# State space output of a hybrid decoder block: unmasked half-height products, put in feature order by DMA

## The chip, the cores and the metric

One core of one Trainium2 chip runs the whole kernel. The metric is the device time of one execution in microseconds (us), as the median of three runs. TensorE is the matrix engine (PE in the rows, its weight loads PEld), VectorE is DVE, ScalarE is ACT, GpSimd is POOL. SyncE (SP) issues every DMA of this kernel, in one queue.

## What is computed

A decoder block over 272 positions (16 meta tokens and 256 real ones) of width 2048. The part that matters is the state space branch (S5): 64 groups of 16 features, each with 64 complex states.

```python
_, _, h_re, h_im = lax.associative_scan(combine, (at_re, at_im, bu_re, bu_im), axis=1)
y = (jnp.einsum('gcp,blgp->blgc', c_re, h_re) - jnp.einsum('gcp,blgp->blgc', c_im, h_im))
y = y.reshape(bsz, L, D_SSM) + d_skip * u
ya, yb = jnp.split(jax.nn.gelu(y) @ w_glu, 2, axis=-1)
ssm_out = ya * jax.nn.sigmoid(yb)
merged = jax.nn.sigmoid(ga) * ssm_out + jax.nn.sigmoid(gb) * attn
```

`ga`, `gb`, `u` and the attention's q, k, v are columns of one projection of the normed input.

## The kernel before, in words

**Main stream.** All large products are split in high and low fp32r halves and take three products (lines L693, L694, L695) for each 128 features of contraction. The weights come in units of 128 x 1024 fp32; one unit is 24 products. Units are numbered through the program: 112 to 143 are the 16 tiles `ps_ga` (two units each), 144 is `ps_ya0`, 145 `ps_yb0`. When unit i begins, `begin_unit` emits the ScalarE cast of unit i+3 (`hi`, L114), the VectorE rest of unit i+2 (`lo`, L129) and the load of unit i+6 (`raw`, L107). There are three `lo` buffers and four each of `raw` and `hi`, so `lo` of unit i+2 cannot start before TensorE has finished unit i-1, and a load cannot start before the `lo` that frees its buffer.

**Background.** Everything else runs in generators. `bg_step` moves each of them on to its next `yield`, in the middle and at the end of each unit. Engines execute in the order in which the instructions are written. The state space generator first brings `u` in the scan's order by 16 DMAs (L541) and forms the inputs of the scan (`pe`, L562), the state `Hs` and a direct matrix `K0` (from `kb`, L578). The scan is 135 steps of four VectorE instructions (L597 to L605), queued in `dvq` and dealt out between the `lo` pieces under a budget for each unit. When the queue is empty and the attention output has been emitted, the output part follows: per block `mt` of 128 features, ScalarE makes a masked copy `ct` of the coefficients (L622), TensorE adds `K0` times `u` (L627) and 16 products of 128 rows by 32 columns (L631), VectorE adds the skip term (`y`, L638), and a gelu in three further steps (L641 to L654) writes `agH` and `agL`, the input of `ps_ya` and `ps_yb`. Steps `t` of this loop are spread over two `yield`s each.

**The join.** After the last `ps_ga`, `force("ssm")` runs whatever is left of the generator without any product of the main stream between, and only then is unit 144 emitted.

```python
    def force(flag):
        while flag not in st:
            spent[0] = 0.0
            while posts and "rstd" in st:
                posts.popleft()()
            while dv():
                pass
            bg_step()
```

Of the kernel before, what the change touches and what calls it, by code (L numbers as in the profile page):

```python
# [9 lines left out]
F32 = mybir.dt.float32  # L10
F32R = mybir.dt.float32r
I32 = mybir.dt.int32
AF = mybir.ActivationFunctionType
ALU = mybir.AluOpType
# [3 lines left out]
P = 128  # L18
# [4 lines left out]
NT = L - T0  # L23
# [5 lines left out]
NJ = L // 2  # L29
J0 = T0 // 2  # L30
NY = NJ - J0
# [6 lines left out]
C_GMIX, C_GFFN, C_CW, C_CB, C_DSK, C_LR, C_LI, C_LDT, C_BF, N_PRM = 0, 16, 32, 164, 208, 216, 248, 280, 312, 313  # L38
# [14 lines left out]
def hybrid_block(tc, hT, wall, wf, prm, cst, bc, gfin, out):  # L53
    nc = tc.nc
    V, A, G, PE = nc.vector, nc.scalar, nc.gpsimd, nc.tensor
    pools = {}

    def open_pool(key, **kw):
        cm = tc.tile_pool(name=key, **kw)
        pools[key] = (cm, cm.__enter__())  # L60
        return pools[key][1]

    def close_pool(key):
        pools.pop(key)[0].__exit__(None, None, None)
# [18 lines left out]
    st = {}  # L83
# [7 lines left out]
    def dv(cost=0.0, gap=0.0):  # L91

        spent[0] += cost
        if dvq and spent[0] + gap + dvq[0][1] <= st.get("budget", BUDGET):
            f, c = dvq.popleft()
            spent[0] += c + gap
            f()
            return True
        return False
# [34 lines left out]
    psb = const.tile([P, N_PRM], F32, name="psb")  # L134
    ident = csb[:, K_ID:K_ID + P]
    glm = csb[:, K_GL:K_GL + 2]
# [30 lines left out]
    u = ssm.tile([P, 8, 2, NJ], F32, name="u")  # L167
    acoef = ssm.tile([P, 4, S_T], F32, name="acoef")
    Bc = ssm.tile([P, 2, S_T, 2, 16], F32, name="Bc")
    Cc = ssm.tile([P, 2, S_T, 2, 16], F32, name="Cc")  # L170
    K0 = ssm.tile([P, 8, P], F32, name="K0")
# [4 lines left out]
    h = pro.tile([P, KT, L], F32, name="h")  # L176
# [347 lines left out]
    def ssm_gen():  # L524
# [10 lines left out]
        Hs = st["hp"].tile([P, 2, S_T, NJ + 1], F32, name="Hs")  # L535
        G.memset(Hs[:, :, :, 0], 0.0)
        for s4 in range(4):
            for g in range(2):
                for ph in range(2):
                    r = 32 * s4 + 16 * ph  # L540
# [15 lines left out]
        for mt in range(8):  # L556
            pes = [st["bgS"].tile([P, 512], F32, tag="bg", name=f"pe{mt}_{s4}") for s4 in range(4)]
            for ri in range(2):
                for g in range(2):
                    for s4 in range(4):  # L560
                        r = slice(32 * s4, 32 * s4 + 32)
# [7 lines left out]
            if mt < 4:  # L569
                ri, g = mt // 2, mt % 2  # L570
# [3 lines left out]
        for mt in range(8):  # L574
            for ri in range(2):
                for s4 in range(4):
                    s = 4 * mt + s4
# [3 lines left out]
        for i in range(4):  # L581
# [2 lines left out]
                         csb[:, K_M16:K_M16 + P].rearrange("p (a c) -> p a c", c=16).unsqueeze(1).broadcast_to([P, 2, 8, 16]))  # L584
            dv(0.35)
        yield
        close_pool("ssmu")
        gbp = open_pool("gbp", bufs=1)
        st["gb"] = gbp.tile([P, KT, NT], F32, name="gb")
# [22 lines left out]
            yield  # L612
        yield
        yp_ = open_pool("ypool", bufs=1)
        cts, pys, ys = {}, {}, {}
        for t in range(8 + 4):
            if t < 8:
                cts[t] = yp_.tile([P, 2, 8, 2, 16], F32, tag="ct", name=f"ct{t}", bufs=2)
                for ri in range(2):
                    src = Cc[:, ri, 4 * t:4 * t + 4].rearrange("p s h c -> p (s h) c")  # L620
                    for g in range(2):
                        A.activation(cts[t][:, ri, :, g, :], src, AF.Copy, scale=glm[:, g:g + 1])  # L622
            if 0 <= t - 1 < 8:
                mt = t - 1
                ct = cts.pop(mt)
                py = st["bgS"].tile([P, 512], F32, tag="bg", name=f"py{mt}")
                PE.matmul(py[:, 0:NY], K0[:, mt, :], u[:, mt, 0, J0:], start=True, stop=False)  # L627
                for ph in range(2):
                    for ri in range(2):
                        for s4 in range(4):  # L630
                            PE.matmul(py[32 * s4:32 * s4 + 32, ph * NY:(ph + 1) * NY],  # L631
                                      ct[:, ri, 2 * s4 + ph].rearrange("p g c -> p (g c)"),
                                      Hs[:, ri, 4 * mt + s4, J0 + ph:NJ + ph], start=ri == 0 and ph == 1, stop=ri == 1)
                pys[mt] = py
            if 0 <= t - 2 < 8:
                mt = t - 2
                y = yp_.tile([P, 2, NY], F32, tag="y", name=f"y{mt}", bufs=3)
                V.scalar_tensor_tensor(y, u[:, mt, :, J0:], psb[:, C_DSK + mt:C_DSK + mt + 1],  # L638
                                       pys.pop(mt)[:, :NT].rearrange("p (h j) -> p h j", h=2), ALU.mult, ALU.add)
                w = yp_.tile([P, 2, NY], F32, tag="w", name=f"w{mt}", bufs=3)  # L640
                A.activation(w, y, AF.Square)  # L641
                ys[mt] = (y, w)
            if 0 <= t - 3 < 8:
                mt = t - 3
                y, w = ys[mt]
                V.tensor_scalar(w, w, 0.044715, 1.0, ALU.mult, ALU.add)
                V.tensor_mul(w, w, y)
                A.activation(w, w, AF.Sigmoid, scale=2.0 * math.sqrt(2.0 / math.pi))
            if 0 <= t - 4 < 8:
                mt = t - 4  # L650
                y, w = ys.pop(mt)
                V.tensor_mul(w, w, y)
                A.copy(agH[:, mt, :].rearrange("p (j h) -> p h j", h=2), w)
                V.tensor_sub(agL[:, mt, :].rearrange("p (j h) -> p h j", h=2), w,  # L654
                             agH[:, mt, :].rearrange("p (j h) -> p h j", h=2).bitcast(F32))
            yield
            yield
# [122 lines left out]
    st["mm"] = open_pool("mm", bufs=2, space=PSUM, reuse_waits="tile")  # L780
    st["bgS"] = open_pool("bgS", bufs=4, space=PSUM, reuse_waits="tile")
    sg = ssm_gen()
    running.extend([forget_gen(), sg])

# [46 lines left out]
    for m in range(KT):  # L831
# [4 lines left out]
        def f(m=m, ps=ps):  # L836
            V.tensor_mul(gb[:, m, :], ps[:, :NT], gb[:, m, :])
# [188 lines left out]
    for k in range(FT - R):  # L1026
        mid_prep(k + 2)
        for half in range(2):
            i = cur[0]
# [160 lines left out]
```

## Time and profile before

| | us |
|---|---|
| median of three runs (lowest, highest) | 1425.29 (1425.01, 1426.26) |
| the profiled execution | 1424.99 |
| its span from the first to the last instruction | 1423.2 |
| TensorE busy in that span | 1403.2 |
| VectorE busy | 975.6 |
| ScalarE busy | 722.7 |

The profiled execution is 1.79 us longer than its span and 0.30 us below the median. A product's busy time is from its start to the modelled end, so products overlap; how fast they follow each other is read from their starts.

### The profile page before, as it was taken

Reading aid. Unit: us, or ns where it says so; the run is one execution under the profiler, and the core shown is the slowest. Engines: PE = TensorE matmul, PEld = TensorE weight load, DVE = VectorE, ACT = ScalarE, POOL = GpSimd, SP = SyncE. Lnnn points to the kernel's source line nnn. Section 1 sums busy time; section 2 is a strip of 40 time slices with the busy share of each in tenths; the row PEclk is TensorE's granted clock in tenths of the full one; section 3 lists DMA queues with packets and bytes.
Section 4 is the critical chain, followed back from the end, with each engine's and each line's share of the span. In section 5 each row is a group of like instructions: output and inputs, shape, how many; then the busy total and the mean of one; then the engine's idle time right before and its main releaser. Section 6 shows DMA issues by size and latency. Waiting matters only on the chain.

```text
span 1423.2 us, 26749 instructions
## 1 busy us (share of the span) xinstructions
PE 1403.2 (99%) x10487; PEld 1319.4 (93%) x10487; DVE 975.6 (69%) x2022; ACT 722.7 (51%) x1147; POOL 56.4 (4%) x80
## 2 busy tenths in 40 slices
PE   8999999999999999999999999999999999999997
PEld 7999999999999999999999999999999998888886
DVE  7887358999998766665766666666666665554565
ACT  5545766644446655555544444444444454444453
POOL 2100000110011000000000000000000000000001
PEclk9999999999999999999999999999999999999999
DMA  8657444555555455765555565565555556555571
GB/s 286 181 177 175 132 147 153 163 170 183 193 166 178 148 181 185 233 198 184 185 187 187 183 188 183 179 189 187 187 188 182 187 183 207 194 191 195 192 243 66
DMA packets 78158, 260.25 MB, mean 183 GB/s; under 512 B 8984, under 2 KB 16336, under 8 KB 77776
## 3 DMA queue, kind: packets, MB, share of 16 engines
q1 hardware_dynamic: 78032, 258.55, 57.2%
q8 instruction: 82, 1.34, 0.4%
q14 instruction: 44, 0.36, 0.1%
HBM read 255.28 MB, written 2.11 MB: 181 GB/s over the span
## 4 chain that ended last, share of the span: by engine, by line
PE 87%; DVE 5%; DMA 1%; ACT 1%; issue 1%; SPq 0%; DVEq 0%; ACTq 0%
PE ps_u L709 11%; PE ps_g L695 6%; PE ps_g L694 6%; PE ps_g L693 6%; PE ps_u L710 6%; PE po L1019 5%; PE po L1021 5%; PE po L1020 5%; PE ps_o L694 2%; PE ps_o L695 2%; DVE lo L129 2%; PE ps_o L693 2%; PE ps_gb L693 2%; PE ps_gb L694 2%; PE ps_gb L695 2%; PE ps_ga L693 1%
## 5 line engine op out<-in xcount | busy, mean ns | idle before, releaser
L129 DVE TENSOR_TENSOR lo<-raw,hi 128x1024 fp32r<-128x1024 f32 (+3 forms) x695 | 608.7, 878 | 244.3 <-PE ps_g L695 102.4
L114 ACT CAST hi<-raw 128x1024 fp32r<-128x1024 f32 x465 | 488.2, 1050 | 472.0 <-PE ps_g L694 143.8
L709 PE MATMUL ps_u<-h2s,hi 128*128 128x512 f32 x704 | 246.2, 393 | 0.0
L695 PE MATMUL ps_g<-h2s,lo 128*128 128x258 f32 x704 | 204.0, 290 | 0.0
L694 PE MATMUL ps_g<-h2L,hi 128*128 128x258 f32 x704 | 198.8, 282 | 0.0
L693 PE MATMUL ps_g<-h2s,hi 128*128 128x258 f32 x704 | 198.2, 282 | 0.0
L710 PE MATMUL ps_u<-h2s,lo 128*128 128x256 f32 x704 | 195.2, 277 | 0.0
L709 PEld LDWEIGHTS ps_u<-h2s,hi 128*128 128x128 f32 x704 | 132.2, 188 | 28.6
L693 PEld LDWEIGHTS ps_g<-h2s,hi 128*128 128x128 f32 x704 | 134.1, 191 | 1.9
L694 PEld LDWEIGHTS ps_g<-h2L,hi 128*128 128x128 f32 x704 | 132.8, 189 | 0.0
L695 PEld LDWEIGHTS ps_g<-h2s,lo 128*128 128x128 f32 x704 | 132.3, 188 | 0.0
L710 PEld LDWEIGHTS ps_u<-h2s,lo 128*128 128x128 f32 x704 | 132.2, 188 | 0.0
L1019 PE MATMUL po<-hi,mH 128*128 128x512 f32 x328 | 127.6, 389 | 0.0
L1021 PE MATMUL po<-hi,mL 128*128 128x512 f32 x328 | 127.6, 389 | 0.0
L1020 PE MATMUL po<-lo,mH 128*128 128x512 f32 x328 | 127.6, 389 | 0.0
L1021 PEld LDWEIGHTS po<-hi,mL 128*128 128x128 f32 x328 | 61.6, 188 | 12.9
L693 PE MATMUL ps_gb<-hgH,hi 128*128 128x258 f32 x256 | 73.5, 287 | 0.0
L693 PE MATMUL ps_o<-hgH,hi 128*128 128x258 f32 x256 | 73.5, 287 | 0.0
L1020 PEld LDWEIGHTS po<-lo,mH 128*128 128x128 f32 x328 | 61.6, 188 | 12.7
L1019 PEld LDWEIGHTS po<-hi,mH 128*128 128x128 f32 x328 | 61.6, 188 | 12.7
L693 PE MATMUL ps_ga<-hgH,hi 128*128 128x258 f32 x256 | 73.2, 286 | 0.0
L694 PE MATMUL ps_gb<-hgL,hi 128*128 128x258 f32 x256 | 72.5, 283 | 0.0
(273 smaller groups left out, 3033.4 us busy)
## 6 DMA issues: line engine op xcount, KB each, us to landing
raw<-in_wall_dram SPq DMA_DIRECT2D x465, 512.0 KB
rawl<-in_wall_dram SPq DMA_DIRECT2D x6, 512.0 KB
hr<-in_hT_dram SPq DMA_DIRECT2D x16, 129.0 KB
h<-in_hT_dram SPq DMA_DIRECT2D x6, 272.0 KB
u<-u SPq DMA_DIRECT2D x16, 68.0 KB
bcs<-in_bc_dram SPq DMA_DIRECT2D x1, 1024.0 KB
gfb<-in_gfin_dram SPq DMA_DIRECT2D x1, 1024.0 KB
out_dram<-h3g SPq DMA_DIRECT2D x6, 128.0 KB
```

The source lines that it names most:

```text
L114: A.copy(his[i], raws[i])
L129: V.tensor_sub(lo[:, a:b], w[:, a:b], hi[:, a:b].bitcast(F32))
L693: PE.matmul(ps[:, :n], hi[:, w], xH[:, k, cols], start=k == 0, stop=False)
L694: PE.matmul(ps[:, :n], hi[:, w], xL[:, k, cols], start=False, stop=False)
L695: PE.matmul(ps[:, :n], lo[:, w], xH[:, k, cols], start=False, stop=k == kts - 1)
L709: PE.matmul(ps, hi[:, w], x[:, k, :], start=k == 0, stop=False)
L710: PE.matmul(ps[:, :NO], lo[:, w], x[:, k, :NO], start=False, stop=k == kts - 1)
L1019: PE.matmul(o, mH[:, t], hi[:, c], start=k == 0, stop=False)
L1020: PE.matmul(o, mH[:, t], lo[:, c], start=False, stop=False)
L1021: PE.matmul(o, mL[:, t], hi[:, c], start=False, stop=last)
```

## The change

The masked copies `ct` are dropped. Each product of the output now takes the 64 rows of one group half (`g`) and 32 columns, and 130 positions, so that both phases come out of one product; the two halves write two PSUM tiles `py0_0`, `py0_1`. The eight blocks are done in three stretches (3, 3 and 2 blocks) instead of one by one. ScalarE copies the result to `yg`, and 32 small DMAs from SP's queue (L652 of the changed kernel) move it in feature order into `yt`, which lies over `K0` and `Bc`. The product with `K0` and the skip term move to part B, in front of the scan (`pk`), where `u` is overwritten by its part of the sum. The gelu steps follow after the DMAs; there the add is now between two SBUF tiles.

```diff
--- before.py
+++ after.py
@@ -584,6 +584,19 @@
                          csb[:, K_M16:K_M16 + P].rearrange("p (a c) -> p a c", c=16).unsqueeze(1).broadcast_to([P, 2, 8, 16]))
             dv(0.35)
         yield
+
+        pks = [st["bgS"].tile([P, 512], F32, tag="bg", name=f"pk{i}") for i in range(3)]
+        for mt in range(8):
+            PE.matmul(pks[mt // 3][:, mt % 3 * NY:(mt % 3 + 1) * NY], K0[:, mt, :], u[:, mt, 0, J0:], start=True, stop=True)
+        yield
+        for mt in range(8):
+            d = psb[:, C_DSK + mt:C_DSK + mt + 1]
+            V.scalar_tensor_tensor(u[:, mt, 0, J0:], u[:, mt, 0, J0:], d, pks[mt // 3][:, mt % 3 * NY:(mt % 3 + 1) * NY],
+                                   ALU.mult, ALU.add)
+            dv(0.2)
+            A.activation(u[:, mt, 1, J0:], u[:, mt, 1, J0:], AF.Copy, scale=d)
+            if mt % 4 == 3:
+                yield
         close_pool("ssmu")
         gbp = open_pool("gbp", bufs=1)
         st["gb"] = gbp.tile([P, KT, NT], F32, name="gb")
@@ -612,31 +625,42 @@
             yield
         yield
         yp_ = open_pool("ypool", bufs=1)
-        cts, pys, ys = {}, {}, {}
-        for t in range(8 + 4):
-            if t < 8:
-                cts[t] = yp_.tile([P, 2, 8, 2, 16], F32, tag="ct", name=f"ct{t}", bufs=2)
+
+        yg = yp_.tile([P, 2, 8, NY + 1], F32, name="yg")
+        flat = (K0.rearrange("p m c -> p (m c)"), Bc.rearrange("p r s h c -> p (r s h c)"))
+        yt = [x[:, :n * 2 * NY].rearrange("p (m h j) -> p m h j", m=n, h=2) for x, n in zip(flat, (3, 5))]
+        for mts in ((0, 1, 2), (3, 4, 5), (6, 7)):
+            py = [st["bgS"].tile([P, 512], F32, tag="bg", name=f"py{mts[0]}_{g}") for g in range(2)]
+            for i, mt in enumerate(mts):
                 for ri in range(2):
-                    src = Cc[:, ri, 4 * t:4 * t + 4].rearrange("p s h c -> p (s h) c")
-                    for g in range(2):
-                        A.activation(cts[t][:, ri, :, g, :], src, AF.Copy, scale=glm[:, g:g + 1])
-            if 0 <= t - 1 < 8:
-                mt = t - 1
-                ct = cts.pop(mt)
-                py = st["bgS"].tile([P, 512], F32, tag="bg", name=f"py{mt}")
-                PE.matmul(py[:, 0:NY], K0[:, mt, :], u[:, mt, 0, J0:], start=True, stop=False)
-                for ph in range(2):
-                    for ri in range(2):
-                        for s4 in range(4):
-                            PE.matmul(py[32 * s4:32 * s4 + 32, ph * NY:(ph + 1) * NY],
-                                      ct[:, ri, 2 * s4 + ph].rearrange("p g c -> p (g c)"),
-                                      Hs[:, ri, 4 * mt + s4, J0 + ph:NJ + ph], start=ri == 0 and ph == 1, stop=ri == 1)
-                pys[mt] = py
-            if 0 <= t - 2 < 8:
+                    for s4 in range(4):
+                        for g in range(2):
+                            r, s = slice(64 * g, 64 * g + 64), 4 * mt + s4
+                            PE.matmul(py[g][32 * s4:32 * s4 + 32, i * (NY + 1):(i + 1) * (NY + 1)],
+                                      Cc[r, ri, s].rearrange("p h c -> p (h c)"), Hs[r, ri, s, J0:], start=ri == 0, stop=ri == 1)
+            yield
+            for g in range(2):
+                A.copy(yg[:, g, mts[0]:mts[-1] + 1].rearrange("p m j -> p (m j)"), py[g][:, :len(mts) * (NY + 1)])
+            yield
+            if mts[0] == 3:
+                continue
+            part = 1 if mts[0] else 0
+            for s4 in range(4):
+                for g in range(2):
+                    for ph in range(2):
+                        r = 32 * s4 + 16 * ph
+                        nc.sync.dma_start(yt[part][32 * s4 + 16 * g:32 * s4 + 16 * g + 16, :, ph, :],
+                                          yg[r:r + 16, g, 3 * part:mts[-1] + 1, ph:ph + NY])
+                if part:
+                    yield
+        yield
+        yield
+        ys = {}
+        for t in range(2, 8 + 4):
+            if t - 2 < 8:
                 mt = t - 2
-                y = yp_.tile([P, 2, NY], F32, tag="y", name=f"y{mt}", bufs=3)
-                V.scalar_tensor_tensor(y, u[:, mt, :, J0:], psb[:, C_DSK + mt:C_DSK + mt + 1],
-                                       pys.pop(mt)[:, :NT].rearrange("p (h j) -> p h j", h=2), ALU.mult, ALU.add)
+                y = yt[mt > 2][:, mt if mt < 3 else mt - 3]
+                V.tensor_add(y, y, u[:, mt, :, J0:])
                 w = yp_.tile([P, 2, NY], F32, tag="w", name=f"w{mt}", bufs=3)
                 A.activation(w, y, AF.Square)
                 ys[mt] = (y, w)
```

Three places show how instructions move. The first is VectorE at the end of the scan; `sp`, `sq` and `Hs` are a scan step, `lo134` the rest of weight unit 134. Before:

```order
L605 TENSOR_TENSOR Hs_1620<-Hs_1620,sq_134_6469 128x64
L597 TENSOR_TENSOR sp135_6477<-Hs_1620,acoef_87 128x64
L598 TENSOR_TENSOR sp135_6477<-Hs_1620,acoef_87 128x64
L602 TENSOR_TENSOR sq_135_6480<-sp135_6477 128x64
L605 TENSOR_TENSOR Hs_1620<-Hs_1620,sq_135_6480 128x64
L129 TENSOR_TENSOR lo135_6517<-raw135_6342,hi135_6461 128x1024
```

And now:

```order
L129 TENSOR_TENSOR lo135_6522<-raw135_6355,hi135_6474 128x336
L618 TENSOR_TENSOR Hs_1620<-Hs_1620,sq_134_6528 128x64
L610 TENSOR_TENSOR sp135_6534<-Hs_1620,acoef_87 128x64
L611 TENSOR_TENSOR sp135_6534<-Hs_1620,acoef_87 128x64
L615 TENSOR_TENSOR sq_135_6537<-sp135_6534 128x64
L129 TENSOR_TENSOR lo136_6566<-raw136_6398,hi136_6520 128x344
L618 TENSOR_TENSOR Hs_1620<-Hs_1620,sq_135_6537 128x64
```

The last state of the scan stood ahead of `lo135`; it now stands behind all of `lo135` and the first third of `lo136`. On TensorE the first output product moved from the end of unit 133 to the end of unit 134.

The second is VectorE ahead of the join; `w6` and `w7` are the gelu of blocks 6 and 7, and `lo146` is emitted when unit 144 (`ps_ya0`) begins. Before:

```order
L654 TENSOR_TENSOR agL_78<-w6_6999,agH_77 128x2x129
L129 TENSOR_TENSOR lo145_7088<-raw145_6887,hi145_7048 128x1024
L652 TENSOR_TENSOR w7_7039<-w7_7039,y7_7037 128x258
L654 TENSOR_TENSOR agL_78<-w7_7039,agH_77 128x2x129
L129 TENSOR_TENSOR lo146_7129<-raw146_6951,hi146_7086 128x1024
```

And now, the first twelve rows from `lo145` on (19 more of the same kind follow, up to `agL` of `w7`, and then `lo146`):

```order
L129 TENSOR_TENSOR lo145_7047<-raw145_6901,hi145_7004 128x1024
L663 TENSOR_TENSOR Bc_88<-Bc_88,u_86 128x258
L670 TENSOR_SCALAR w2_7037<-w2_7037 128x258
L671 TENSOR_TENSOR w2_7037<-w2_7037,K0_90 128x258
L676 TENSOR_TENSOR w1_6998<-w1_6998,K0_90 128x258
L678 TENSOR_TENSOR agL_78<-w1_6998,agH_77 128x2x129
L663 TENSOR_TENSOR Bc_88<-Bc_88,u_86 128x258
L670 TENSOR_SCALAR w3_7076<-w3_7076 128x258
L671 TENSOR_TENSOR w3_7076<-w3_7076,Bc_88 128x258
L676 TENSOR_TENSOR w2_7037<-w2_7037,K0_90 128x258
L678 TENSOR_TENSOR agL_78<-w2_7037,agH_77 128x2x129
L663 TENSOR_TENSOR Bc_88<-Bc_88,u_86 128x258
```

Between `lo145` and `lo146` there were two instructions, and there are now 31: the adds of blocks 3 to 7 and `agL` of blocks 1 to 7.

The third is SP's queue over the same units, now (before, the loads `raw141` to `raw149` followed each other with nothing between):

```order
L107 DMA raw141_6657<-in_wall_dram 128x1024
L652 DMA K0_90<-yg_6602 16x3x129 x16
L107 DMA raw142_6756<-in_wall_dram 128x1024
L107 DMA raw143_6824<-in_wall_dram 128x1024
L652 DMA Bc_88<-yg_6602 16x5x129 x4
L107 DMA raw144_6861<-in_wall_dram 128x1024
L652 DMA Bc_88<-yg_6602 16x5x129 x8
L107 DMA raw145_6901<-in_wall_dram 128x1024
L652 DMA Bc_88<-yg_6602 16x5x129 x4
L107 DMA raw146_6936<-in_wall_dram 128x1024
```

Loads 142 to 146 now stand behind 16 to 32 small DMAs.

## Rows read from the trace of the kernel before

**Rows 1.** Windows: stretch, its length, busy time by engine, granted clock, DMA.

```profile
130.00:205.00 75.00, 73.12 (x895) 68.78 (x895) 32.07 (x61) 52.28 (x125) 2.29 (x9) 1.00 0.50 153
381.00:440.00 59.00, 59.00 (x496) 59.00 (x495) 57.13 (x200) 23.77 (x30) 8.21 (x9) 1.00 0.54 175
```

**Rows 2.** Timeline of TensorE around output products and the join: start, duration, instruction, count.

```profile
443.75 0.28 PE L695 MATMUL ps_ga<-hgH,lo 128*128 128x258 f32 x1
...
444.44 0.65 PE L631 MATMUL py<-Hs,ct 128*32 128x129 f32 x16 [0.18 <-ACT ct L622]
...
446.13 0.28 PE L694 MATMUL ps_ga<-hgL,hi 128*128 128x258 f32 x1
...
448.76 0.28 PE L695 MATMUL ps_ga<-hgH,lo 128*128 128x258 f32 x1
448.88 0.39 PE L627 MATMUL py<-u,K 128*128 128x129 f32 x2
449.20 1.09 PE L631 MATMUL py<-Hs,ct 128*32 128x129 f32 x32
...
450.44 0.29 PE L694 MATMUL ps_ga<-hgL,hi 128*128 128x258 f32 x1
...
484.86 0.28 PE L693 MATMUL ps_ya<-agH,hi 128*128 128x258 f32 x1
...
487.72 0.28 PE L693 MATMUL ps_yb<-agH,hi 128*128 128x258 f32 x1
```

**Rows 3.** Timeline of TensorE around one batch of `pe`.

```profile
146.19 0.29 PE L695 MATMUL ps_k<-hgH,lo 128*128 128x272 f32 x1
146.41 0.72 PE L562 MATMUL pe<-u,bt 32*64 32x136 f32 x32
...
147.29 0.29 PE L694 MATMUL ps_k<-hgL,hi 128*128 128x272 f32 x1
```

**Rows 4.** Timeline of VectorE at the end of the scan.

```profile
442.19 0.51 DVE L129 TENSOR_TENSOR lo<-raw,hi 128x344 fp32r<-128x344 f32 x1
...
445.00 0.27 DVE L605 TENSOR_TENSOR Hs<-Hs,sq 128x64 f32<-128x64 f32 x1
```

**Rows 5.** Timeline of VectorE: one rest of a unit, then one gelu step.

```profile
474.99 1.22 DVE L129 TENSOR_TENSOR lo<-raw,hi 128x1024 fp32r<-128x1024 f32 x1 [0.41 <-PE ps_ga L695]
476.26 0.48 DVE L638 SCALAR_TENSOR_TENSOR y<-u,psb,py 128x258 f32<-128x258 f32 x1
476.66 0.29 DVE L646 TENSOR_SCALAR w<-w 128x258 f32<-128x258 f32 x1
476.99 0.43 DVE L647 TENSOR_TENSOR w<-w,y 128x258 f32<-128x258 f32 x1
477.33 0.42 DVE L652 TENSOR_TENSOR w<-w,y 128x258 f32<-128x258 f32 x1
478.24 0.43 DVE L654 TENSOR_TENSOR agL<-w,agH 128x258 fp32r<-128x258 f32 x1 [0.49 <-ACT agH L653]
```

**Rows 6.** Timeline of SP's queue at the 16 DMAs that reorder `u`.

```profile
119.38 5.20 SPq L541 DMA_DIRECT2D u<-u  x8
...
125.69 6.83 SPq L541 DMA_DIRECT2D u<-u  x8
```

**Rows 7.** Critical chain, 118 to 140 us: start, length, what.

```profile
125.30 6.62 DMA raw<-in_wall_dram
```

**Rows 8.** Timeline of TensorE at the start of the program.

```profile
4.46 0.57 PE L756 MATMUL pu<-hgH,hi 128*128 128x272 f32 x1 [4.46 <-DVE hi L126]
...
9.36 0.43 PE L758 MATMUL pu<-hgH,lo 128*128 128x272 f32 x1
9.59 0.43 PE L756 MATMUL pu<-hgH,hi 128*128 128x272 f32 x1
```

**Rows 9.** Windows behind the last product.

```profile
1413.00:1414.00 1.00, 0.99 (x5) 1.00 0.81 282
...
1416.00:1417.00 1.00, 0.00 (x0) 0.63 0.00 0
```

## The prediction

> **What bounds the kernel now.** I read the windows first. In the stretch of the last `ps_ga` tiles TensorE is busy for all 59.00 us, and VectorE for 57.13 of 59.00 [rows 1]: TensorE sets the time, and VectorE, which deals out the scan between the rests `lo`, has hardly any room. So the timeline of TensorE prices whatever it does, and the timelines of VectorE and SP say whether it is kept waiting. Before the change it is not kept waiting at the join: the first `ps_ya` product starts at 484.86 and the first `ps_yb` at 487.72 [rows 2], one unit of 24 products in 2.86 us, 0.119 us each.
>
> **What is removed.** One output batch goes from the last `ps_ga` product ahead of it (448.76) to the second behind it (450.44): 1.68 us, of which two pitches (0.24) would be there anyway, so 1.44 [rows 2]. Seven cost 10.1. The first also waits for the scan: 446.13 less 443.75 less 0.24 is 2.14 [rows 2]. Together **-12.2 us**. The masked copies on ScalarE and the drains into another array shape go too; the drains are inside these numbers.
>
> **The new products.** There are as many passes per block, 32, but eight tiles of the array can be at work instead of four. In the old batch 16 passes take 0.65 and 32 take 1.09 [rows 2]: four more rounds of four cost 0.44, a round 0.11. The nearest row for eight at once is `pe` (32 rows by 64 columns): 32 passes, four rounds, move the main stream by 147.29 - 146.19 - 0.24 = 0.86 [rows 3], edges included. A stretch of three blocks is 12 rounds, 0.86 + 8 x 0.11 = 1.74; the last, 8 rounds, 1.30. Sum **+4.8**. Bounds: 4.5 if the edges are smaller; 5.8 if every four rounds cost the 0.65 between the starts at 146.41 and the next main product, as in `pe`, and each stretch 0.2 of edges.
>
> **`K0` in part B.** The same 16 passes move ahead of the scan. In the old batch the pair goes from 448.88 to 449.20 [rows 2], 0.32 with a change of shape, 0.12 per pass without. Taken **+2.0** (1.9 to 2.2). The eight skip adds on 129 columns are about 0.3 us each (an estimate: `y` on 258 takes 0.48 [rows 5]), eight ScalarE scales likewise. In that stretch VectorE is busy 32.07 and ScalarE 52.28 of 75.00 us [rows 1], so they hide: 0. Without that cover it would be 2.4.
>
> **The scan's end comes later than the product that needs it.** The rest of unit 134 is emitted when unit 132 begins. Unit 132 begins two units (5.7 us) ahead of the 443.87 at which unit 133 is through, at 438.1, but VectorE comes to that rest at 442.19 [rows 4]: it is four us behind, and still so as long as the scan lasts. The last state is written at 445.00 [rows 4], 1.1 us behind `ps_ga`'s end; that wait is inside the 2.14. Now the first product stands one unit later, but the last state behind the first third of `lo136`. With the same lag that rest starts 4.1 us after unit 134 begins, that is 1.2 after it ends; with 0.51 for the third and 0.27 for the add TensorE waits about **+2.1**. Bounds: 1.0, as before, if the lag melts by a us; 2.6 if it grows.
>
> So far -12.2 + 4.8 + 2.0 + 2.1 = -3.3 us.
>
> **The join.** Call P the moment at which TensorE is through with the last `ps_ga` and could start `ps_ya0`. The DMAs and the longer pipeline use 32 generator steps instead of 24, and the output begins a unit later, so that only blocks 0 to 2 have had their add when unit 143 ends. Seven gelu steps are left and run with no main product between them, while `ps_ya0` needs one block every three products and all eight by its 23rd product, P + 22 x 0.119 = P + 2.6.
> VectorE's queue: `lo144` starts when unit 141 is through and frees a buffer, P - 5.72, and takes 1.27 to the next start [rows 5]. A full gelu step takes 1.98 from the add to the start of `agL`, then 0.43, less an overlap of some 0.08: 2.33 [rows 5]. In it VectorE waits 0.49 for ScalarE's `agH`. So the step behind `lo144` ends at P - 2.12, `lo145` at P - 0.85, and five full steps at P + 10.8; one without an add (1.93) at P + 12.7; the last (0.42 + 0.49 + 0.43) at P + 14.1. TensorE gets its last block 11.5 us late. Nothing behind can give this back, since TensorE is the bound there too.
> The 32 small DMAs lengthen it. SP issues eight such in 5.20 us, once in 6.83 [rows 6], 0.65 each, so loads 145 and 146 stand behind 28 and 32 of them, 18 and 21 us. A load among them took 6.62 from issue to landing [rows 7]. Counting from the first small DMA (2.6 us into the first stretch, P - 28), load 146 is issued near P - 5.3 and lands near P - 1 to P + 1.3; its cast stands ahead of the remaining squares on ScalarE, so the chain may start 0 to 4 us later. I take 0.5: **+12.0** (11.5 to 15.5).
>
> **The clock.** During the join TensorE does three products every 2.3 us. Behind the last product of the program, which ends by 1414, the granted clock falls between 1416 and 1417 [rows 9], from 2.4 to 1.2 GHz; nothing before shows bursts this sparse. At the start, from 4.46 to 9.59, products are 0.23 apart instead of 0.12 [rows 8]: some 22 products at 0.11 too much, 2.4 us. So the clock costs 0 (if it holds) to 2.4. The join is nearer to idle than to work: **+2.0**. The Trainium skill's page "TensorE: Matmul & The Clock Gate" (Part 1) calls the throttled state the default that activity lifts; the trace agrees at both ends.
>
> **Sum:** 1424.99 - 3.3 + 12.0 + 2.0 = **1435.7 us**. The ends of all terms together are 1431.7 and 1441.3. Against the median of 1425.29 it would be 0.3 less of a loss.
>
> **Rivals.** Likeliest (0.62): as above, 1433 to 1439.
> *The clock holds and the scan's wait stays at 1.0* (0.16): 1431.7 to 1433.
> *The small DMAs become the queue's bound* (0.08): if they wait for each other, loads 145 and 146 come 5 us or more later than reckoned, `lo145` with them, and the join costs 17 or more: 1441 and up. For it speaks 6.83 for the second eight, against it 5.20 for the first. The Trainium skill's "DMA: Bandwidth & Descriptors" (Rules for kernel authors) speaks against the change: transfers under 64 KB are mostly overhead; these have 24.8 and 41.3 KB. Its fit, 2.0 us and a little per DMA, would by itself be an estimate of some 66 us one after another, which would put the time tens of us higher; eight issues in 5.20 us speak against that reading (0.01 of the 0.08).
> *The two row halves do not run side by side* (0.05): 16 to 24 rounds per stretch instead of 8 to 12, 28 more rounds at 0.11, 3.1 us: 1438.8.
> *Same* (0.05): VectorE overlaps successive steps so that only its 31 instructions count, about 0.34 each, 10.5 us from P - 0.85: the join then costs 7.1, and with the clock holding, no wait at the scan and the cheap end of the products 1427 to 1428.
> *Faster* (0.04): the gelu steps are no obstacle because the adds, squares and casts run ahead of `lo145`. It decides at 3.3 us of join: all seven steps would have to fit in 6.8 us instead of 15. Fully hidden it gives 1421.7. Against it stands VectorE's order, which puts 31 instructions behind `lo145`.
>
> Slower by over 0.2% (2.9 us, about what a measurement of this kernel can tell from no change): 0.91. Range 1430.5 to 1440.5: it leaves out the two best cases and the DMA case.
>
> **What would show it.** Right: `ps_ya0`'s products in groups of three about 2.3 us apart, TensorE waiting for `agH` and `agL` for 11 to 15 us in all; VectorE with 31 instructions between two rests; a lower granted clock behind the join; TensorE's first `py0` product waiting some 2 us for `Hs`; rounds of eight passes in 0.11. Wrong: no wait at `ps_ya0`, or loads landing so late that TensorE waits for `hi` or `lo` elsewhere.

## The result and the profile after

The changed kernel takes 1466.96 us (median of five runs, 1465.75 to 1467.63) against 1425.29: a ratio of 1.029 [1.028, 1.030]. It was forecast slower, but at 1435.7; 31 us of the loss were not in the sum.

The waits of TensorE over the whole span (us in total, times, longest). Of those above 1 us these three are new:

```profile
PE ps_ya L717 <- ACT agH L677: 25.6, 7, 14.4
PE ps_ga L717 <- ACT hi L114: 8.1, 1, 8.1
...
PE py L639 <- DVE Hs L618: 2.2, 1, 2.2
```

TensorE lacks a cast weight (`hi`) in the middle of `ps_ga`, which the prediction did not have, and the gelu's output at the join, as forecast but with one wait of 14.4. Both go back to SP. Its queue over those units, which answers to [rows 6] (start, time, line, count):

```profile
453.41 25.93 SPq L652 DMA_DIRECT2D K<-yg  x16
479.38 1.06 SPq L107 DMA_DIRECT2D raw<-in_wall_dram  x2
480.49 7.97 SPq L652 DMA_DIRECT2D Bc<-yg  x4
...
489.12 12.68 SPq L652 DMA_DIRECT2D Bc<-yg  x8
...
502.48 6.86 SPq L652 DMA_DIRECT2D Bc<-yg  x4
```

The 32 small DMAs keep SP for 25.93 + 7.97 + 12.68 + 6.86 = 53.4 us, 1.67 each, where 0.65 each was reckoned. A weight load written behind them (`raw`, 479.38) goes out 26 us after the first of them. SP's own waits in that stretch say why:

```profile
SPq L652 <- DMA Bc<-yg: 17.5, 8, 3.9
SPq L652 <- DMA K<-yg: 15.0, 8, 3.5
```

Sixteen times, at every second small DMA, SP waits for an earlier small DMA to land, 32.5 us in all; 53.4 less 32.5 is 20.9, just the 32 x 0.65 of the sum. The chain of waits shows the beat (a landing is counted from the start of the issue): the first of a pair is issued and lands, then the second is issued, then the first of the next pair.

```profile
464.96 1.94 DMA K<-yg
466.93 0.58 SPq L652
...
467.55 1.94 DMA K<-yg
469.50 0.58 SPq L652
```

The second DMA of a pair (`ph` = 1) writes the same 16 partitions of `yt` as the first, into columns that lie between those of the first (`[..., :, ph, :]`: for each block 129 of one phase, then 129 of the other). The program makes it wait for its twin; `e1` below tests this. That it goes by the columns in between and not by the shared partitions shows in `e10`, where the phases lie apart in the target: there the two of the first pair go out 0.1 us apart, from two queues, and neither waits for the other.

What it does downstream stands in the timelines of ScalarE and VectorE (in brackets the idle time and what ended it):

```profile
483.27 1.04 ACT L114 CAST hi<-raw 128x1024 fp32r<-128x1024 f32 x1 [17.20 <-DMA raw<-in_wall_dram]
...
505.70 1.04 ACT L114 CAST hi<-raw 128x1024 fp32r<-128x1024 f32 x1 [11.19 <-DMA raw<-in_wall_dram]
```

```profile
484.35 1.23 DVE L129 TENSOR_TENSOR lo<-raw,hi 128x1024 fp32r<-128x1024 f32 x1 [15.34 <-ACT hi L114]
...
507.99 0.43 DVE L678 TENSOR_TENSOR agL<-w,agH 128x258 fp32r<-128x258 f32 x1 [11.50 <-ACT agH L677]
```

A cast waits for its load and, since engines work in order, the gelu's `agH` stands behind that cast, and `agL` behind `agH`. TensorE's timeline, answering to [rows 2]:

```profile
449.91 2.85 PE L639 MATMUL py<-Hs,Cc 64*32 64x130 f32 x96 [2.21 <-DVE Hs L618]
...
455.97 1.62 PE L639 MATMUL py<-Hs,Cc 64*32 64x130 f32 x96
...
508.01 0.58 PE L717 MATMUL ps_ya<-agH,hi 128*128 128x258 f32 x1 [14.35 <-ACT agH L677]
```

And the window of the join (columns as in [rows 1]; the number before the last two is the granted clock):

```profile
485.00:530.00 45.00, 18.92 (x75) 15.04 (x75) 20.72 (x46) 15.38 (x33) 2.87 (x3) 0.58 0.27 84
```

`ps_ya` starts at 508.0 instead of 484.86 [rows 2]. No engine is the bound from 485 to 530: TensorE is busy 18.92 of 45 us, VectorE 20.72, at a mean granted clock of 0.58 (0.50 would be the lower level, 1.2 GHz, throughout).

### The profile page after: what moved, and what is told of

Same layout as the page of the kernel before. It is cut to its first block, busy times and chain, and to the rows that moved or that the text cites. A ratio compares the mean times of both kernels' runs of the same rounds, so it can differ in the third digit from the quotient of the medians.

```text
span 1465.5 us, 26798 instructions
## 1 busy us (share of the span) xinstructions
PE 1410.8 (96%) x10487; PEld 1324.4 (90%) x10487; DVE 976.4 (67%) x2032; ACT 718.3 (49%) x1129; POOL 56.2 (4%) x80
## 3 DMA queue, kind: packets, MB, share of 16 engines
HBM read 255.28 MB, written 2.11 MB: 176 GB/s over the span
## 4 chain that ended last, share of the span: by engine, by line
PE 64%; DMA 3%; DVE 1%; ACT 1%; SPq 1%; issue 0%; DVEq 0%; ACTq 0%
PE ps_u L733 11%; PE ps_g L719 6%; PE ps_g L718 6%; PE ps_g L717 6%; PE ps_u L734 6%; PE po L1043 5%; PE po L1044 5%; PE po L1045 5%; PE ps_o L718 2%; PE ps_o L719 2%; PE ps_o L717 2%; DMA K<-yg 1%; PE ps_yb L718 1%; PE ps_yb L717 1%; PE ps_yb L719 1%; PE ps_ya L717 1%
## 5 line engine op out<-in xcount | busy, mean ns | idle before, releaser
L718 PE MATMUL ps_g<-h2L,hi 128*128 128x258 f32 x704 | 198.8, 282 | 0.0
L733 PEld LDWEIGHTS ps_u<-h2s,hi 128*128 128x128 f32 x704 | 132.2, 188 | 28.6
L718 PE MATMUL ps_ga<-hgL,hi 128*128 128x258 f32 x256 | 73.6, 288 | 0.0
L719 PE MATMUL ps_ga<-hgH,lo 128*128 128x258 f32 x256 | 73.1, 285 | 0.5 <-DVE lo L129 0.5
```

The lines of the kernel that those rows point to most:

```text
L718: PE.matmul(ps[:, :n], hi[:, w], xL[:, k, cols], start=False, stop=False)
L719: PE.matmul(ps[:, :n], lo[:, w], xH[:, k, cols], start=False, stop=k == kts - 1)
L733: PE.matmul(ps, hi[:, w], x[:, k, :], start=k == 0, stop=False)
```

## The experiments

Twelve kernels, in three groups of four, each group on one chip beside the kernel before (medians there 1425.62, 1424.80 and 1424.67).

### 1. The twins kept apart (`e1_twins_apart`)

All first phases are issued ahead of all second phases; nothing else moves.

```diff
-            for s4 in range(4):
-                for g in range(2):
-                    for ph in range(2):
+            for ph in range(2):
+                for s4 in range(4):
+                    for g in range(2):
...
-                if part:
-                    yield
+                    if part and s4 % 2:
+                        yield
```

> The changed kernel with the 32 small DMAs in another order: all of the first phase, then all of the second, so that the two that write interleaved columns of the same 16 partitions are eight apart instead of next to each other. Theory W (each second small DMA waits for its twin to land, which makes SP's queue 53 us long and the loads late): 16 issues take about 10.5 us instead of 25.9, no wait of TensorE for hi, the join costs 12 to 14 us, time 1434 to 1439. Rival R (small pieces are slow in the DMA engines whatever the order): unchanged, 1464 to 1469. Rival C (the clock that falls in the 2.2 us wait at py0 starts it all): about 1467 too, since that wait stays.

Measured 1438.32 us, ratio 1.009 [1.007, 1.011]: 28.6 us of the loss came from the waits between twins. SP's queue now:

```profile
452.28 12.22 SPq L652 DMA_DIRECT2D K<-yg  x16
...
465.69 2.58 SPq L652 DMA_DIRECT2D Bc<-yg  x4
...
468.94 6.09 SPq L652 DMA_DIRECT2D Bc<-yg  x8
...
475.70 2.51 SPq L652 DMA_DIRECT2D Bc<-yg  x4
```

23.4 us for the 32, 0.73 each, with the same bytes, number and size. The cause of the miss is shown, and this run is the test of the rest of the sum (below).

### 2. No small DMAs at all (`e2_no_small_dma`)

The 32 DMAs are left out, their `yield`s stay; the gelu then works on old contents of the buffers.

> The changed kernel without the 32 small DMAs (the output of the scan never reaches the gelu; the yields stay). Theory W: what is left is the join, within 2 us of the run with the twins apart, 1433 to 1438. Rival R: 1433 to 1438 as well, but then far below the run with the twins apart. Rival C: about 1467.

Measured 1435.62, ratio 1.0075 [1.0055, 1.0095], 2.7 below `e1` (within 2 was expected): in this order of the gelu steps the DMAs, once they don't wait for each other, cost little.

### 3. The join's wait taken away (`e3_no_join_wait`)

On top of `e1`, the first three pairs `ps_ya`, `ps_yb` multiply eight blocks of `hgH`, `hgL` in place of `agH`, `agL`, so they wait for no gelu (other numbers come out).

```diff
-        tile_mm(psa, agH, agL, H, slice(0, NT))
+        glu_in = (hgH[:, 8:, :], hgL[:, 8:, :], H, tail) if m < 3 else (agH, agL, H, slice(0, NT))
+        tile_mm(psa, *glu_in)
...
-        tile_mm(psb_, agH, agL, H, slice(0, NT))
+        tile_mm(psb_, *glu_in)
```

> The twins apart, and the first three pairs of ps_ya and ps_yb tiles read the normed input instead of the gelu output, so that TensorE has no wait at the join (the numbers of those tiles are others). Theory J (the gelu steps left over at the join cost 12 to 14 us there and nothing else is lost): 1421 to 1425, at or below the kernel before. Rival: the steps cost VectorE and ScalarE time that shows later, 1430 or more.

Measured 1435.39, ratio 1.007 [1.005, 1.009]: a miss. TensorE now waits two units later, for a weight rest:

```profile
PE ps_ya L719 <- DVE lo L129: 12.8, 1, 12.8
```

`lo146` stands behind the 31 gelu instructions in VectorE's order (the change section shows it). So the price is that of VectorE's queue, whoever asks first.

### 4. The direct term alone (`e4_direct_term_only`)

The kernel before, with only the part B edit: `K0`'s product and the skip term ahead of the scan, the masked copies and the blocks as before.

> The kernel before with only the direct term moved to part B (pk, skip term in place; masked products, one block at a time, no DMAs). Expected by the rows: +1.8 us for pk in part B, -2.6 us for eight pairs of 0.32 in the output part: 1424 to 1425.5, the same as before. Rival: the scan starts later and ends behind its first product, as in the changed kernel, and the pipeline of blocks runs past the join: 1428 to 1432.

Measured 1423.82, ratio 0.9986 [0.9977, 0.9996]: below the kernel before, by less than the 0.2% that the prediction counts as a change. In part B, the stage ahead of the scan, the 16 passes show as forecast (`pk`, 2.0 reckoned):

```profile
204.37 1.95 PE L590 MATMUL pk<-u,K 128*128 128x129 f32 x16
```

### 5 to 8. Gelu earlier (`e5` to `e8`)

In `e1` VectorE is busy for 13 of the 30 us ahead of the join (the third number of the window):

```profile
450.00:480.00 30.00, 30.00 (x451) 28.98 (x438) 13.12 (x17) 11.40 (x19) 2.90 (x3) 1.00 0.56 154
```

These four put the gelu there; `e5` builds on `e1` and each of the others on the one before. `e5`: the first small DMAs beside the second stretch, the rest four at a time beside the first gelu steps.

```diff
+        move(0, 0, range(4))
+        py = stretch((3, 4, 5))
+        yield
+        move(0, 1, range(4))
+        drain((3, 4, 5), py)
...
+            for _ in range(2):
+                if moves:
+                    move(*moves.pop(0))
+                yield
```

> The twins stay apart, and the gelu steps begin six generator steps earlier: the first small DMAs go out beside the second stretch, those of blocks 3 to 7 four at a time beside the first gelu steps, so that three gelu steps fewer are forced at the join (four instead of seven). Theory V (VectorE's idle room): in the run with the twins apart VectorE is busy for 13 of the 30 us from 450 to 480, so the three steps find room there and the join loses 3 x 2.3 = 7 us: 1430 to 1432.5. Rival F (VectorE is as good as full, as the windows of the kernel before had it; steps moved forward push the rests lo back, and TensorE waits for lo instead): 1436 to 1439. Rival L (late loads 145 and 146 set the join, not the steps): 1436 to 1439 as well, but with the wait at ps_ya0's first product and few forced steps behind it.

`e6`: one `yield` instead of two behind each step from the third on.

> As the run with gelu earlier, and from the third gelu step on each step takes one generator step instead of two, so that none is left to be forced at the join. Theory V: from the first gelu step near 460 to ps_ya0's last block near 484 VectorE has 24 us; six rests take 7.6 and eight blocks 18.6, 26.2 together, 2.4 too many, so some of the join stays: 1421.5 to 1425. Rival F: two steps stand ahead of each lo, 5.9 us of VectorE's work for 2.86 of TensorE's, and TensorE waits for lo in units 140 to 146: 1428 and up.

`e7`: `agL` of a block one step later.

```diff
-                V.tensor_sub(agL[:, mt, :].rearrange("p (j h) -> p h j", h=2), w,
...
+                ws[mt] = y
+            if 0 <= t - 5 < 8:
+                mt = t - 5
+                V.tensor_sub(agL[:, mt, :].rearrange("p (j h) -> p h j", h=2), ws.pop(mt),
```

> As the run with one yield, and agL of a block stands one step later in VectorE's order, so that the wait of 0.49 for ScalarE's agH in each step goes (eight times, 3.9 us of VectorE's time). Theory V: 22.3 us of work in 24, nothing left at the join: 1421 to 1422.5, that is up to 3 below the run with one yield, and 0 below it if nothing was left there. Rival F: as the run with one yield less 1 to 4, still above 1425.

`e8`: two `yield`s ahead of the first stretch.

> As the run without the wait for agH, and the first stretch one unit (two generator steps) later, so that the scan's last state is there when it starts: no gap of 2.2 us on TensorE. Theory C (the half-speed first stretch, 2.85 us instead of 1.56, comes from the clock, which fell in the gap): the stretch takes 1.5 to 1.6 and the time falls by 2.2 + 1.3 = 3.5, to 1417.5 to 1419, unless the output, 2.9 us later, no longer fits ahead of the join (then some 2.4 of it comes back there). Rival S (the first stretch is slow by itself, being the first of its kind): it takes 2.8 again, 1419 to 1420.

Measured 1439.76 [1.0094, 1.0124], 1438.16 [1.0080, 1.0106], 1434.28 [1.0056, 1.0086] and 1437.70 [1.0072, 1.0097]. `e5` to `e7` miss theory V, though `e7` forces almost nothing at the join. `e8` misses theory C's time: it is 3.4 slower than `e7` where 3.5 less was forecast. Its wait for the scan is gone, but the later output costs more at the join (8.2 us of waits for `agL` against 1.9). VectorE's waits in `e7` from 440 to 500:

```profile
DVE Bc L674 <- DMA Bc<-yg: 6.5, 1, 6.5
DVE K L674 <- DMA K<-yg: 6.5, 1, 6.5
```

The room is there, but the data isn't: the add stands in VectorE's queue 6.5 us ahead of its DMAs, and the rests behind it are late (TensorE waits 6.8 for a `lo`). SP issues from 453.55 on and puts out the last four small DMAs where `e1` does (475.70):

```profile
476.85 2.51 SPq L651 DMA_DIRECT2D Bc<-yg  x4
```

So two things reach the join at about the same time, the gelu steps of VectorE and the issues of SP, and taking away either alone (`e2` the second, `e5` to `e7` the first) leaves the other.

### 9 to 12. Both taken away (`e9` to `e12`)

`e9`: `e7` without its 32 small DMAs (old buffer contents again).

> The run without the wait for agH, with its 32 small DMAs left out (the gelu then works on what lies in the buffers, so the numbers are not those of the block). Theory S (two obstacles lie side by side: SP issues the small DMAs until about 479 whatever the order, and the gelu steps of VectorE come late; taking away one leaves the other, which is why the run without small DMAs in the changed order and the run with the earlier gelu both stayed above 1430): with both away the join is hidden, 1421 to 1424. Rival F (VectorE's order alone sets it): 1430 to 1434, TensorE waiting for lo and agL as in the run with the DMAs.

Measured 1425.24, ratio 1.0002 [0.9993, 1.0011], 1.2 above theory S's range. With both away the join is nearly hidden; each alone had left 9 us or more.

`e10`: all the DMAs, the second phase from GpSimd's queue; the phases apart in the target; the stretches one `yield` apart.

```diff
+        yt = [x[:, :n * 2 * (NY + 1)].rearrange("p (h m j) -> p m h j", m=n, h=2) for x, n in zip(flat, (3, 5))]
...
+                    (nc.gpsimd if q else nc.sync).dma_start(
+                        yt[part][d:d + 16, :, q, :].rearrange("p m j -> p (m j)")[:, :n * (NY + 1) - 1],
...
+            for _ in range((1, 2, 2, 2, 1, 2, 1, 1, 1, 1, 1)[t - 2]):
+                yield
```

> All 32 small DMAs again, half of them (the second phase) from GpSimd's queue; the two phases lie apart in the target, the stretches follow each other by one generator step and the eleven gelu steps begin four steps after the first stretch, laid out so that the last falls on the end of unit 143. Theory S: SP issues 16 instead of 32, each half beside the other, the last lands by 470 and the gelu of block 3 (near 466 to 468) waits 0 to 3 us for it: 1421 to 1424.5. Rival P (an issue from GpSimd's queue takes well over 0.65 us, or stands behind GpSimd's own work, so the DMAs land near 478 again): 1428 to 1434.

`e11`: the same with `nc.sync` for both phases.

> As the run with two queues, but all 32 small DMAs from SP's. Theory S: 32 issues at 0.65 to 0.78 and three or four loads take SP from 452 to 476 or 479; five blocks at 1.7 and two rests behind the last landing put the last block near 491 to 493, 7 to 9 us late: 1428 to 1433. Rival O (the new order of the gelu steps is what counts, not the queue): as the run with two queues.

`e12`: `e10` with two `yield`s ahead of the first stretch and two fewer among the gelu steps.

> The run with two queues, and the first stretch one unit later, so that it does not wait for the scan's end. The 2.2 to 2.4 us wait goes, and in runs where the clock fell behind it another 0.7 to 1.3; the gelu steps have one unit less. Theory S: 1418.5 to 1422, 1 to 3.5 below the run with two queues. Rival (VectorE has no room for the same steps in one unit less: 2.9 us of it comes back at the join): as the run with two queues, or 1 slower.

Measured: `e10` 1425.95, ratio 1.0013 [1.0004, 1.0022]; `e11` 1436.99, 1.0078 [1.0064, 1.0092]; `e12` 1428.23, 1.0024 [1.0014, 1.0034]. `e10` and `e11` differ in the queue alone: it is worth 11.0 us. As times all three lie above theory S's ranges, by 1.5, 4.0 and 6.2. In `e10` SP's and GpSimd's parts of the small DMAs run side by side, first SP's timeline, then GpSimd's:

```profile
452.16 6.02 SPq L652 DMA_DIRECT2D K<-yg  x8
...
458.90 5.84 SPq L652 DMA_DIRECT2D Bc<-yg  x8
```

```profile
452.26 4.02 POOL L652 DMA_DIRECT2D K<-yg  x8 [4.98 <-ACT yg L645]
...
458.29 3.90 POOL L652 DMA_DIRECT2D Bc<-yg  x8
```

All are out by 464.7, 13.5 us ahead of `e1`. In `e11` the last leaves SP at 478.0 (start and length of the second row):

```profile
454.67 11.79 SPq L652 DMA_DIRECT2D K<-yg  x16
...
467.18 10.79 SPq L652 DMA_DIRECT2D Bc<-yg  x16
```

At the join of `e10` TensorE still waits twice, then runs most of `ps_yb` at half speed (granted clock 0.50 from 488 to 490); the timeline, with the starts of `ps_ya0`, `ps_yb0` and the next `ps_ya`:

```profile
480.37 0.28 PE L732 MATMUL ps_ya<-agH,hi 128*128 128x258 f32 x1
...
483.71 0.39 PE L733 MATMUL ps_ya<-agL,hi 128*128 128x258 f32 x1 [1.03 <-DVE agL L693]
...
485.64 0.39 PE L733 MATMUL ps_ya<-agL,hi 128*128 128x258 f32 x1 [1.31 <-DVE agL L693]
...
486.45 0.28 PE L732 MATMUL ps_yb<-agH,hi 128*128 128x258 f32 x1
...
490.83 0.28 PE L732 MATMUL ps_ya<-agH,hi 128*128 128x258 f32 x1
```

From 480.37 to 490.83 are 10.46 us for two units that take 5.72 at [rows 2]'s pace: 4.7 too many, some 3.2 in the first and 1.5 in the second (486.45 to 490.83 is 4.38). `ps_ya0` starts 480.37 - 199.55 = 280.82 us behind the batch `kb` of part B, which lies ahead of everything changed; before it was 484.86 - 200.39 = 284.47. So 3.6 are saved ahead of the join and 4.7 lost in it, and 1.1 is about what `e10` is slower.

`e12` is 2.3 slower than `e10`, the rival's way, but by more than its 1:

```profile
479.49 0.28 PE L734 MATMUL ps_ya<-agH,hi 128*128 128x258 f32 x1
...
492.20 0.28 PE L734 MATMUL ps_ya<-agH,hi 128*128 128x258 f32 x1
```

Its first two units take 12.71 us instead of 10.46, and with `kb` at 198.84 `ps_ya0` starts 280.65 behind it, no earlier than in `e10`: the wait for the scan is gone, but other delays of the stretches and of `ps_ga` have taken its place (TensorE stands 0.94 us in the third stretch; why stays open). No version beats the kernel before by more than 0.2%; `e4` is the lowest.

## Why the prediction was wrong

**The step that failed** is in the join: "SP issues eight such in 5.20 us, once in 6.83 [rows 6], 0.65 each, so loads 145 and 146 stand behind 28 and 32 of them, 18 and 21 us". The price of an issue was right (0.58 in the chain above, 0.65 with what lies between), but it was taken as the whole price of a DMA: they cost 53.4 us in SP's queue, not 20.8. The `u` DMAs from which the price came go into places of their own; these come in pairs on the same partitions, with columns in between each other's, and each second one waits for a landing too. The pairs are in the diff (`ph` is the innermost loop), and at the chain's shortest beat, 467.55 - 464.96 = 2.59 us for a pair, sixteen pairs would have made 41 us. The rival *The small DMAs become the queue's bound*, "if they wait for each other", named the mechanism at 0.08. It weighed it by a row of other DMAs, and the 6.83 in that row was no sign of it: SP's waits in the kernel before show 1.5 us there for a weight load.

```profile
SPq L541 <- DMA raw<-in_wall_dram: 1.5, 1, 1.5
```

Its "1441 and up" was the right side with no upper end worked out, and the reading that it gave 0.01, all 32 one after another in some 66 us, was nearer to the 53.4 than the sum was. The prediction's own sign of being wrong, loads so late that TensorE waits for `hi` elsewhere, came with the wait of 8.1 us. The Trainium skill's "DMA: Bandwidth & Descriptors" (Rules for kernel authors) calls transfers under 64 KB mostly overhead. The trace agrees: 24.8 KB land in 1.94 us at the shortest and 41.3 KB in 2.11, so the bytes make little of it. The overhead holds up the queue where the next DMA waits for it (1.67 us each); where none waits, only the issue is paid (0.73).

**With that taken away** (`e1`), the other terms can be read. The main stream up to the join: -3.3 forecast. The batch `kb`, ahead of everything changed, starts at 200.39 before and 198.98 in `e1`:

```profile
198.98 1.27 PE L578 MATMUL kb<-Cc,Bc 128*32 128x16 f32 x128
...
449.45 1.62 PE L639 MATMUL py<-Hs,Cc 64*32 64x130 f32 x96 [2.34 <-DVE Hs L618]
...
453.87 0.28 PE L719 MATMUL ps_ga<-hgH,lo 128*128 128x258 f32 x1
454.07 1.62 PE L639 MATMUL py<-Hs,Cc 64*32 64x130 f32 x96
...
455.85 0.29 PE L718 MATMUL ps_ga<-hgL,hi 128*128 128x258 f32 x1
...
481.37 0.39 PE L717 MATMUL ps_ya<-agH,hi 128*128 128x258 f32 x1 [1.31 <-ACT agH L677]
...
498.60 0.42 PE L717 MATMUL ps_yb<-agH,hi 128*128 128x258 f32 x1
...
503.16 0.28 PE L717 MATMUL ps_ya<-agH,hi 128*128 128x258 f32 x1
```

```profile
200.39 1.27 PE L578 MATMUL kb<-Cc,Bc 128*32 128x16 f32 x128
```

(the second fence is the kernel before). From `kb` to the moment at which `ps_ya0` could start are 481.37 - 1.31 - 198.98 = 281.08 us, before 484.86 - 200.39 = 284.47: -3.4. A stretch of three blocks moves the stream by 455.85 - 453.87 - 0.24 = 1.74, as reckoned from `pe`; the wait for the scan's end is 2.34 (2.1 forecast). The half arrays do run side by side. (Two side sums and a reading of the prediction are off. The rival that they do not reckons 28 more rounds; its own counts make 32, 3.5 us. The terms of the rival *Same* add up to 1426.4, not 1427 to 1428. And the window from 381 to 440 in [rows 1] is the first part of `ps_ga`, in which the scan runs, and not its last tiles: from 440 to 485 VectorE was busy 33.93 of 45.00 us before. None of this changes the sum.)

**The join and the clock**: 14.0 forecast. In `e1` the first two units behind P = 480.06 take until 503.16, 23.1 us for 5.72: 17.4. The forecast put the start of the chain of gelu steps 0.5 late, with 0 to 4 as its ends; the last rest ahead of it starts at 481.70 instead of P - 2.12 = 477.94, 3.8 late, because `agH` stands behind a cast that waits for its load. ScalarE first, then VectorE:

```profile
479.07 1.05 ACT L114 CAST hi<-raw 128x1024 fp32r<-128x1024 f32 x1 [3.72 <-DMA raw<-in_wall_dram]
```

```profile
481.35 0.43 DVE L678 TENSOR_TENSOR agL<-w,agH 128x258 fp32r<-128x258 f32 x1 [4.03 <-ACT agH L677]
481.70 1.22 DVE L129 TENSOR_TENSOR lo<-raw,hi 128x1024 fp32r<-128x1024 f32 x1
```

So this term was taken 3.3 too small, which is nearly all of the difference between 14.0 and 17.4. `e2`, where there are no small DMAs, bears it out: there P is 485.55, the same rest starts 0.5 behind P - 2.12, and the first two units take 14.5 too long.

```profile
483.95 1.22 DVE L129 TENSOR_TENSOR lo<-raw,hi 128x1024 fp32r<-128x1024 f32 x1
```

The steps themselves came as forecast, 2.26 us apart against 2.33 (from 487.56 to 489.82 in `e1`), and the clock near the 2.0 taken: `ps_yb0` alone takes 503.16 - 498.60 - 2.86 = 1.7 too long.

The two parts, -3.4 and 17.4, make 14.0 for `e1`; its span is only 12.6 longer, because that execution came to `kb` 1.4 sooner. In the profiled executions `kb` starts anywhere from 198.8 to 203.1, with nothing changed ahead of it, so that much is chance.

**"Nothing behind can give this back"** held: in `e1` 503.16 is 12.6 behind 490.58 (487.72 + 2.86 [rows 2]), and so are the spans, 1435.8 and 1423.2. **The "faster" rival** asked that all gelu steps run ahead of the join; `e9` and `e10` nearly bring that about and come within 0.13% of the kernel before, not below it: two waits of about 1 us and the clock behind them (4.7 in `e10`) take what was saved.

## What to carry to other kernels

Price a DMA by its issue only if nothing behind it in the queue needs its landing, and look at the targets of neighbours: of two that write columns between each other's, on the same partitions, the second waited here for the first, and 32 of them cost 53 us instead of 23. Where several things reach the same join (steps of one engine, issues of another), one experiment on each finds each of them free; only both together show the price. A queue that issues many small DMAs among weight loads can be a bound of its own, and a second queue was worth 11 us here.

## What the runs showed of the hardware

- **The clock behind a short gap.** In the kernel after, TensorE stands for 2.21 us and the first stretch then takes 2.85 us (granted clock 0.50 from 450 to 452); the same 96 passes take 1.62 further on. In `e5` a gap of 2.10 gives 2.34, in `e2` 2.22 gives 2.43, in `e11` 2.33 gives 2.85; in `e1` 2.34 (granted clock 1.00), `e7` 2.36 and `e10` 2.21 leave 1.62. With no gap (`e8`) it is 1.62 too. So such a gap may cost up to 1.2 us more through the clock, and its length within this range does not tell whether; what does stays open.
- **GpSimd's queue** put out eight small DMAs in 3.90 to 4.02 us, 0.5 each, SP's in 5.84 to 6.02. They land later: 4.8 to 4.9 us from the issue (the median of eight in `e10`) against 1.94 to 3.8 for those of SP's queue in the chain of the kernel after, where they went one or two at a time. The Trainium skill's "DMA: Bandwidth & Descriptors" (Issuing engines are not separate DMA queues) says that several issuing engines save only the time of issue, usually small beside the transfer. Here that time counted: `e11` less `e10` is 11.0 us.
